# Gate and up of a hybrid block: stores issued from POOL's queue, raw weights asked for one projection ahead

## The chip, the core and the metric

The kernel runs on one core of a Trainium2 chip. Its time is device microseconds (us) of one execution. The engines are TensorE (PE, with its weight loads PEld), VectorE (DVE), ScalarE (ACT), GpSimd (POOL) and SyncE (SP). SP computes nothing here: it issues DMA transfers in the order of its program, and when an instruction waits on it, the ones behind wait too. POOL can issue transfers in the same way from a queue of its own.

## The reference

One layer of a trunk with two groups of heads, on 2048 tokens of width 1024. Here it is cut to the feed-forward part, in which the change lies; ahead of it a state-space layer and chunked attention share one input and one output projection.

```python
def rmsnorm(x, g):
    return x * lax.rsqrt(jnp.mean(x * x, axis=-1, keepdims=True) + EPS) * g

# D_MODEL = 1024, SEQ = 2048, D_FF = 2816
x = x + mixed @ w_out                       # x1 in the kernel
h = rmsnorm(x, norm_ffn_g)
x = x + (silu(h @ w_gate) * (h @ w_up)) @ w_down
out = rmsnorm(x, norm_final_g)
```

## The kernel before

Everything is float32. Each operand of a product is split into a high part (an ACT cast) and a low part (a DVE subtraction; `split`, L179), and three matmuls (high by high, low by high, high by low) make up one float32 product (`mm3`, L81 in the profile).

**Gate and up** (`gate_up_phase`) goes over two halves of 1024 tokens (`hf`), and in each over 11 pairs of 128-wide blocks of D_FF (`f`, with f + 11), for w_gate and then w_up: 44 *projections*. One projection is a 2 x 2 block product done with seven products instead of eight, called B11, T1, T2, B21, T3, B22 and T4. Their weight operands are made by DVE from two tiles of raw weights, r0 and r1 (512 KB each): sums in S tiles (five of them), split into c tiles (five). The token operands are hi0 to hi6 and lo0 to lo6, one pair for each product; for the second half they are loaded from a buffer in DRAM, `hc` (`build`, L1468), when the first half's last use of the tiles is over. Results gather in three kinds of PSUM banks, X, Y and W; ACT copies some to u tiles. A projection's work is in three parts, and the last part of one is done inside the next: `p.one()`, `before.three()`, `p.two()`.

The raw tiles come in turn from two pools, `k.gr` and `g2`: two pairs in all. Their loads are issued on SP when a `Proj` is made, and each waits for the last reader of the tile.

Beside the projections, a generator (`pre`) is moved on by one step a projection. It first makes the second half's token operands: `pre_steps` loads blocks of x into `px` tiles (four of them, L1428), scales and combines them on DVE, and stores the results to `hc` (L1421). Then `weight_steps` does the same with w_down: loads into px tiles (L1385), combines, and stores to `wc` (L1379). The gated product g (ten tiles) is combined and stored to `hq` (L1575), and the blocks listed in `TAILF` are stored to `hs` as they are (L1571). So hc, wc, hq and hs are buffers in DRAM that are written here and read later.

**Down** (`down_phase`) loads the `hq` and `wc` blocks as hd tiles (768 KB each, a pair for a product), splits them, multiplies into `ps` banks, and adds onto `acc`, tiles loaded from x. Of the first group of blocks, all 14 hd loads are issued from POOL (`aside`); later ones from SP. Their first loads and the acc loads begin while gate and up is ending.

The order on each engine is made by a scheduler from the order of the code; a tile's next user waits for its last reader.

Of the kernel before, what the change touches and what calls it, by code (L numbers as in the profile page):

```python
# [16 lines left out]
P = 128  # L17
# [44 lines left out]
F2 = NF // 2  # L62
# [8 lines left out]
TAILF = 9, 10, 20, 21  # L71
# [1289 lines left out]
def in_turn(n, load, first, second):  # L1361
    for q in range(n + 1):
        if q:
            second(q - 1)
        if q < n:
            load(q)
            yield
            first(q)
        yield


def weight_steps(k, S, tile, tile1):

    nc = k.nc
    V = nc.vector
    st = {}

    def put(f, n, a):
        nc.sync.dma_start(S["wc"][f, n], a[:])  # L1379

    def load(f):
        st[f] = []
        for r, c in ((0, 0), (0, 1), (F2, 0), (F2, 1)):
            a = tile()
            nc.sync.dma_start(a[:], k.io["w_down"][(f + r) * P : (f + r + 1) * P, c * 512 : (c + 1) * 512])  # L1385
            st[f].append(a)

    def first(f):
        a11, a21, a12, a22 = st[f]
        for n, a in ((B11, a11), (B21, a12), (T4, a22)):  # L1390
            put(f, n, a)
        s1 = tile1()
        V.tensor_tensor(s1[:], a21[:], a22[:], op=ALU.add)
        put(f, T1, s1)
        V.tensor_tensor(a21[:], a11[:], a21[:], op=ALU.subtract)
        put(f, T3, a21)
        st[f].append(s1)

    def second(f):
        a11, _, a12, _, s1 = st.pop(f)  # L1400
        V.tensor_tensor(a11[:], s1[:], a11[:], op=ALU.subtract)
        put(f, T2, a11)
        V.tensor_tensor(a12[:], a12[:], a11[:], op=ALU.subtract)
        put(f, B22, a12)

    for m, f in enumerate(TAILF):
        k.tc.keep_in_program_order(nc.sync.dma_start(S["wt"][m], k.io["w_down"][f * P : (f + 1) * P, :]))
    yield from in_turn(F2, load, first, second)


def pre_steps(k, S, hf, tile, deep, tile1=None):

    nc = k.nc
    V = nc.vector
    t0 = hf * HALF
    st = {}

    def put(q, n, b):  # L1420
        nc.sync.dma_start(S["hc"][hf, n, :, q], b)  # L1421

    def load(q):
        st[q] = []
        for r, c in ((0, 0), (0, 1), (4, 0), (4, 1)):
            b = tile()[:]
            ts = slice(t0 + c * 512, t0 + c * 512 + 512)
            nc.sync.dma_start(b, S["x1"][(q + r) * P : (q + r + 1) * P, ts])  # L1428
            st[q].append((b, q + r, ts))

    def first(q):
        for b, r, ts in st[q]:
            V.scalar_tensor_tensor(b, b, k.gf[:, r : r + 1], S["rsn"][:, ts], op0=ALU.mult, op1=ALU.mult)
        b11, b12, b21, b22 = st[q] = [b for b, _, _ in st[q]]
        for n, b in ((B11, b11), (B21, b21), (B22, b22)):
            put(q, n, b)
        t = (tile1 or tile)()[:]
        V.tensor_tensor(t, b12, b11, op=ALU.subtract)
        put(q, T1, t)
        V.tensor_tensor(b12, b22, b12, op=ALU.subtract)  # L1440
        put(q, T3, b12)
        st[q].append(t)

    def second(q):
        b11, b12, b21, b22, t = st.pop(q)
        V.tensor_tensor(b22, b22, t, op=ALU.subtract)
        put(q, T2, b22)
        V.tensor_tensor(b21, b21, b22, op=ALU.subtract)
        put(q, T4, b21)

    if deep:
        for q in range(6):
            for d, f in ((2, second), (1, first), (0, load)):
                if 0 <= q - d < 4:
                    f(q - d)
            yield
    else:
        yield from in_turn(4, load, first, second)


def build(k, S, hf, pool, ns):

    hT = {}
    for n in ns:
        hi, lo = hT[n] = tuple(k.t(pool, f"{m}{n}", [P, 4, 512], F32R) for m in ("hi", "lo"))
        with k.tc.high_priority():
            for q in range(4) if hf == 0 else (slice(0, 4),):
                k.nc.sync.dma_start(f32(lo[:, q]), S["hc"][hf, n, :, q])  # L1468
        for q in range(4):
            split(k, hi[:, q], lo[:, q], f32(lo[:, q]))  # L1470
    return hT


def gate_up_phase(k, S):

    tc, nc, io = k.tc, k.nc, k.io
    V, te = nc.vector, k.te
    with ExitStack() as cx:
# [9 lines left out]
        xr = rstd_steps(k, te, psum["X"], k.mf, ("X", [P, 512]), k.last, D, S["rsn"][:, (NSB - 1) * SB :])  # L1488

        raws = cycle((k.gr,) * 2 + (g2,) * 2)  # L1490

        class Proj:


            def __init__(self, hT, w, f, post):
                self.hT, self.post = hT, post
                r0, r1 = (k.t(next(raws), "raw", [P, 1024]) for _ in range(2))
                nc.sync.dma_start(r0[:], w[f])
                nc.sync.dma_start(r1[:], w[f + F2])
                self.a11, self.a12, a21, self.a22 = r0[:, :512], r0[:, 512:], r1[:, :512], r1[:, 512:]  # L1500

                def s(x, y, op):
                    o = k.t(gb, "S", [P, 512], bufs=SB_)
                    V.tensor_tensor(o[:], x, y, op=op)
                    return o[:]

                self.s1 = s(a21, self.a22, ALU.add)
                self.s2 = s(self.s1, self.a11, ALU.subtract)
                self.s3 = s(self.a11, a21, ALU.subtract)
                self.s4 = s(self.a12, self.s2, ALU.subtract)  # L1510
# [34 lines left out]
            def three(self):  # L1545
                self.product(B22, self.s4, self.y, False)
                self.add(self.u2, self.y, 0, 1)
                self.product(T4, self.a22, self.x, False)
                self.post(self.x, 1, 0)

        before = None
        tiles = (lambda: k.t(gp, "px", [P, 512])), (lambda: k.t(gb, "S", [P, 512], bufs=SB_))
        pre = chain(pre_steps(k, S, 1, tiles[0], False, tiles[1]), weight_steps(k, S, *tiles))
        for hf in range(2):
            hT = build(k, S, 1, k.ga1, EARLY) if hf else k.hT
            hT.update(build(k, S, hf, ga, LATE))
            for f in range(F2):
                gs = {}

                def gt():  # L1560
                    return k.t(gb, "g", [P, 512], bufs=GB_)

                def gate(u, r, c, gs=gs):
                    g = gs[r, c] = gt()
                    nc.scalar.activation(g[:], u[:], AF.Silu)

                def up(u, r, c, gs=gs, hf=hf, f=f):
                    g = gs[r, c]
                    V.tensor_tensor(g[:], g[:], u[:], op=ALU.mult)
                    if hf and f + r * F2 in TAILF:  # L1570
                        nc.sync.dma_start(S["h"][TAILF.index(f + r * F2), :, c * 512 : (c + 1) * 512], g[:])  # L1571
                        return

                    def put(n, b):
                        nc.sync.dma_start(S["hq"][hf, f, n], b[:])  # L1575

                    if (r, c) == (0, 0):
                        put(B11, g)
                    elif (r, c) == (1, 1):
                        put(B22, g)  # L1580
                    elif (r, c) == (0, 1):
                        t1, t2 = gt(), gt()
                        V.tensor_tensor(t1[:], g[:], gs[0, 0][:], op=ALU.subtract)
                        put(T1, t1)
                        V.tensor_tensor(t2[:], gs[1, 1][:], t1[:], op=ALU.subtract)
                        put(T2, t2)
                        V.tensor_tensor(g[:], gs[1, 1][:], g[:], op=ALU.subtract)
                        put(T3, g)
                        gs["t2"] = t2
                    else:  # L1590
                        put(B21, g)
                        t4 = gt()
                        V.tensor_tensor(t4[:], g[:], gs["t2"][:], op=ALU.subtract)
                        put(T4, t4)

                for w, post in (("w_gate", gate), ("w_up", up)):
                    p = Proj(hT, io[w], f, post)
                    p.one()
                    if before:
                        before.three()  # L1600
                    p.two()
                    before = p
                    if hf or f > 1:
                        next(pre, None)
                if hf == 0 and f < 2:
                    next(xr)
# [284 lines left out]
```

## Time and profile before

| | |
|---|---|
| median of 3 runs | 2211.99 us (2210.46 to 2216.73) |
| profiled execution, own time | 2214.67 us |
| its span | 2212.9 us |
| mean granted clock of PE | 0.992 |
| PE busy | 2155.7 us, 97% |
| DVE busy | 1534.3 us, 69% |
| ACT busy | 1008.1 us, 46% |
| POOL busy | 371.5 us, 17% |
| moved by the hardware queue (SP) | 404.05 MB |
| moved by the software queue (POOL) | 25.24 MB |

Times in the views are microseconds from the start of the span, which leaves some 1.8 us of the execution outside. In a timeline row stand start, length, engine, line, operation, output<-input and count, and in square brackets how long the engine was idle before and what it waited for. A merged row (x2 and more) runs to the end of its last instruction. In a row of stretches the granted clock (1.00 is full) stands behind the engines. SPq is SP's queue: the length of a row there is the issue, not the transfer.

### The profile page before, as it was taken

To read this page: it belongs to the slowest core of one execution; us is meant where nothing else is said; L and a number is where in the kernel's file an instruction comes from. 1 tells how busy PE (TensorE), PEld (TensorE's weight loads), DVE (VectorE), ACT (ScalarE), POOL (GpSimd) and SP (SyncE) were. 2 spreads that over 40 slices of the span, in tenths; PEclk is the share of its full clock that TensorE was granted. 3 is DMA by queue.
4 is the path that set the end of the run, shared out by engine and by line. 5 is a ranking of instruction groups with operands and counts; after the bars stand their busy time and mean duration, and the time that the engine had idled before them with its cause. 6 is when DMAs were issued, how large, how long until landed. Compare 5 with 4: busy or idle time off the path is not lost.

```text
span 2212.9 us, 30057 instructions
## 1 busy us (share of the span) xinstructions
PE 2155.7 (97%) x10606; PEld 1816.1 (82%) x10606; DVE 1534.3 (69%) x2667; ACT 1008.1 (46%) x1684; POOL 371.5 (17%) x839
## 2 busy tenths in 40 slices
PE   8999999999998999999999999999999999999998
PEld 6787898998977888788888887888888788888887
DVE  8767566565568657767776768767665477689785
ACT  6356566555677521533333345333333443354332
POOL 3367777676110000000000000000000100000000
PEclk9999999999999999999999999999999999999999
DMA  9788977665633346835555657545332395465552
GB/s 323 240 284 268 303 229 241 210 202 174 202 111 138 119 143 218 262 100 182 177 174 190 211 189 262 194 159 203 110 113 102 123 390 179 164 220 197 193 216 77
DMA packets 194423, 431.20 MB, mean 195 GB/s; under 512 B 19744, under 2 KB 37200, under 8 KB 187168
## 3 DMA queue, kind: packets, MB, share of 16 engines
q1 hardware_dynamic: 186448, 404.05, 54.7%
q0 software_dynamic: 7824, 25.24, 3.8%
q8 instruction: 83, 1.36, 0.3%
q14 instruction: 68, 0.56, 0.1%
HBM read 290.00 MB, written 131.10 MB: 190 GB/s over the span
## 4 chain that ended last, share of the span: by engine, by line
PE 61%; DMA 5%; DVE 2%; ACT 1%; issue 1%; SPq 0%; DVEq 0%; ACTq 0%
PE X L81 21%; PE ps L81 17%; PE Y L81 11%; PE big L81 6%; PE W L81 5%; DMA acc<-x 2%; DMA lo<-hc 1%; DMA x<-xt 1%; DVE xt L1239 0%; DMA hd<-wc 0%; DMA m<-in_w_out 0%; ACT hi L179 0%; DMA hc<-gh 0%; DVE acc L1664 0%; SPq L1134 0%
## 5 line engine op out<-in xcount | busy, mean ns | idle before, releaser
L81 PE MATMUL X<-hi,c 128*128 128x512 f32 x1408 | 451.7, 392 | 9.6 <-DVE c L179 5.0
L81 PE MATMUL ps<-hd,hd 128*128 128x512 f32 (+1 forms) x1920 | 428.8, 384 | 3.4 <-DVE hd L179 2.0
L81 PEld LDWEIGHTS ps<-hd,hd 128*128 128x128 f32 x1920 | 353.3, 188 | 75.1 <-DVE hd L179 2.7
L81 PEld LDWEIGHTS X<-hi,c 128*128 128x128 f32 x1408 | 265.8, 189 | 66.5 <-DVE c L179 5.9
L81 PE MATMUL X<-lo,c 128*128 128x512 f32 x704 | 275.3, 391 | 0.0
L179 ACT CAST hd<-hd 128x1536 fp32r<-128x1536 f32 (+1 forms) x106 | 147.5, 1394 | 230.7 <-DMA hd<-hq 164.9
L81 PE MATMUL Y<-hi,c 128*128 128x512 f32 x704 | 224.8, 390 | 1.5 <-DVE u L1526 1.5
L179 DVE TENSOR_TENSOR hd<-hd 128x1536 fp32r<-128x1536 f32 (+1 forms) x106 | 174.2, 1645 | 35.9 <-ACT hd L179 35.1
L179 DVE TENSOR_TENSOR c<-S,c 128x512 fp32r<-128x512 f32 x176 | 120.9, 688 | 101.0 <-ACT c L179 100.8
L1630 POOL DMA_DIRECT2D hd<-hq x7 | 5.2, 745 | 1072.0 <-PE X L81 1060.7
L1522 ACT COPY u<-X 128x512 f32<-128x512 f32 x132 | 77.4, 587 | 197.7 <-PE X L81 197.7
L179 ACT CAST c<-S 128x512 fp32r<-128x512 f32 x176 | 109.4, 622 | 121.7 <-PE Y L81 62.0
L81 PE MATMUL big<-m,woh 128*128 128x512 f32 x512 | 161.2, 396 | 0.0
L81 PEld LDWEIGHTS Y<-hi,c 128*128 128x128 f32 x704 | 132.7, 189 | 29.9 <-DVE u L1526 2.2
L1664 DVE TENSOR_TENSOR acc<-acc,ps 128x512 f32<-128x512 f32 x196 | 130.3, 683 | 38.5 <-PE ps L81 38.0
L81 PEld LDWEIGHTS X<-lo,c 128*128 128x128 f32 x704 | 132.9, 189 | 27.5
L179 ACT CAST c<-raw 128x512 fp32r<-128x512 f32 x132 | 82.2, 623 | 148.8 <-PE Y L81 73.0
L81 PE MATMUL pf<-hi,w 128*128 128x512 f32 x416 | 148.8, 410 | 0.0
L81 PE MATMUL Y<-lo,c 128*128 128x512 f32 x352 | 137.2, 390 | 0.0
L957 DVE TENSOR_TENSOR ptl<-pt,pth 128x640 fp32r<-128x640 f32 (+3 forms) x152 | 98.3, 646 | 46.1 <-ACT pth L956 42.1
L940 ACT ACTIVATE s<-s,mn 128x640 f32<-128x640 f32 (+4 forms) x128 | 97.9, 765 | 51.4 <-DVE mn L937 50.9
L956 ACT CAST pth<-pt 128x640 fp32r<-128x640 f32 (+3 forms) x152 | 83.8, 551 | 81.2 <-PE pt L84 75.7
(494 smaller groups left out, 4281.3 us busy)
## 6 DMA issues: line engine op xcount, KB each, us to landing
w<-wss SPq DMA_DIRECT2D x36, 1024.0 KB, 6.1
hq<-g SPq DMA_DIRECT2D x140, 256.0 KB, 2.1
hd<-hq SPq DMA_DIRECT2D x35, 768.0 KB, 4.4
hd<-wc SPq DMA_DIRECT2D x35, 768.0 KB, 5.9
raw<-in_w_gate SPq DMA_DIRECT2D x44, 512.0 KB, 3.6
raw<-in_w_up SPq DMA_DIRECT2D x44, 512.0 KB, 4.1
wc<-px SPq DMA_DIRECT2D x66, 256.0 KB, 3.1
wss<-w SPq DMA_DIRECT2D x12, 1024.0 KB, 6.3
```

Of the source, the lines that this page charges most:

```text
L81: return self.tc.keep_in_program_order(self.tc.nc.tensor.matmul(*a, **b))
L179: return nc.scalar.copy(hi, raw), nc.vector.tensor_tensor(lo, raw, f32(hi), op=ALU.subtract)
L940: nc.scalar.activation(s[:, :nk], s[:, :nk], AF.Exp, bias=mn[:], scale=-1.0, accum_out=sums[sb, pr][:, hh, qp : qp + 1])
L956: nc.scalar.copy(pth[:, a:b, qp, :], pt[:, a:b, :])
L957: k.low = nc.vector.tensor_tensor(ptl[:, a:b, qp, :], pt[:, a:b, :], f32(pth[:, a:b, qp, :]), op=ALU.subtract).ins
L1522: nc.scalar.copy(u[:], ps[:])
L1630: (nc.gpsimd if aside else nc.sync).dma_start(f32(lo), src.rearrange("g p c -> p g c"))
L1664: V.tensor_tensor(a, a, ps[:], op=ALU.add)
```

## The change

All stores in gate and up (wc, hc of the second half, hq, hs) are issued from POOL instead of SP. The raw weights of a projection are asked for by `load_next()`: once at the start, once behind the first `p.one()`, and from then on at the end of each `three()`; a `Proj` takes the pair that was loaded. The pools and the number of tiles are what they were.

```diff
 def weight_steps(...)
     def put(f, n, a):
-        nc.sync.dma_start(S["wc"][f, n], a[:])
+        nc.gpsimd.dma_start(S["wc"][f, n], a[:])
...
 def pre_steps(...)
     def put(q, n, b):
-        nc.sync.dma_start(S["hc"][hf, n, :, q], b)
+        (nc.gpsimd if hf else nc.sync).dma_start(S["hc"][hf, n, :, q], b)
...
 def gate_up_phase(k, S)
         raws = cycle((k.gr,) * 2 + (g2,) * 2)
+        wanted = iter([(io[n], f) for _ in range(2) for f in range(F2) for n in ("w_gate", "w_up")])
+        loaded = []
+
+        def load_next():
+            for w, f in islice(wanted, 1):
+                r0, r1 = (k.t(next(raws), "raw", [P, 1024]) for _ in range(2))
+                nc.sync.dma_start(r0[:], w[f])
+                nc.sync.dma_start(r1[:], w[f + F2])
+                loaded.append((r0, r1))
 
         class Proj:
-            def __init__(self, hT, w, f, post):
+            def __init__(self, hT, post):
                 self.hT, self.post = hT, post
-                r0, r1 = (k.t(next(raws), "raw", [P, 1024]) for _ in range(2))
-                nc.sync.dma_start(r0[:], w[f])
-                nc.sync.dma_start(r1[:], w[f + F2])
+                r0, r1 = loaded.pop()
...
             def three(self):
                 ...
                 self.product(T4, self.a22, self.x, False)
+                load_next()
                 self.post(self.x, 1, 0)
 
+        load_next()
         before = None
...
                     if hf and f + r * F2 in TAILF:
-                        nc.sync.dma_start(S["h"][...], g[:])
+                        nc.gpsimd.dma_start(S["h"][...], g[:])
                     ...
                     def put(n, b):
-                        nc.sync.dma_start(S["hq"][hf, f, n], b[:])
+                        nc.gpsimd.dma_start(S["hq"][hf, f, n], b[:])
...
-                for w, post in (("w_gate", gate), ("w_up", up)):
-                    p = Proj(hT, io[w], f, post)
+                for post in (gate, up):
+                    p = Proj(hT, post)
                     p.one()
                     if before:
                         before.three()
+                    else:
+                        load_next()
                     p.two()
```

The order of PE and of ACT is the same before and after. On DVE 28 instructions change places with a neighbour. SP's list goes from 1063 to 810 rows, POOL's from 815 to 1068: 253 stores. Lines move by up to 11 (hs L1580, hq L1584, raw L1497 and L1498, hd L1641, acc L1680 after).

On POOL, at the end of gate and up, stand first the loads of the down product's first group (hd, from hq and wc, in pairs). Before:

```order
L1630 DMA hd_16997<-hq_75 128x3x512
L1630 DMA hd_17001<-wc_76 128x3x512
L1630 DMA hd_17005<-hq_75 128x3x512
L1630 DMA hd_17009<-wc_76 128x3x512
L1630 DMA hd_17057<-hq_75 128x3x512
```

Now, with the numbers of the g tiles:

```order
L1580 DMA hs_73<-g_16511 128x512
L1580 DMA hs_73<-g_16571 128x512
L1580 DMA hs_73<-g_16592 128x512
L1580 DMA hs_73<-g_16765 128x512
L1641 DMA hd_16997<-hq_75 128x3x512
L1641 DMA hd_17001<-wc_76 128x3x512
L1641 DMA hd_17005<-hq_75 128x3x512
L1641 DMA hd_17009<-wc_76 128x3x512
L1580 DMA hs_73<-g_16785 128x512
L1580 DMA hs_73<-g_16845 128x512
L1580 DMA hs_73<-g_16862 128x512
L1641 DMA hd_17057<-hq_75 128x3x512
```

Five stores of hs (the first is left out) stand ahead of the first load, and three more between the fourth and the fifth.

On SP at the change of halves (lo: the second half's token operands, here lo4, lo5 and lo6). Before:

```order
L1468 DMA lo4_2617_13642<-hc_10_72 128x2048
L1575 DMA hq_13_75<-g_2578_13418 128x512
L1575 DMA hq_13_75<-g_2581_13438 128x512
L1379 DMA wc_14_76<-S_2646_13824 128x512
L1379 DMA wc_14_76<-px_2605_13591 128x512
L1499 DMA raw_2648_13830<-in_w_up 128x1024
L1468 DMA lo5_2619_13653<-hc_10_72 128x2048
L1468 DMA lo6_2621_13664<-hc_10_72 128x2048
```

Now:

```order
L1468 DMA lo_2619_13646<-hc_72 128x2048
L1498 DMA raw_13761<-in_w_up 128x1024
L1385 DMA px_13974<-in_w_down 128x512
L1385 DMA px_13976<-in_w_down 128x512
L1497 DMA raw_13908<-in_w_gate 128x1024
L1468 DMA lo_2621_13657<-hc_72 128x2048
L1468 DMA lo_2623_13668<-hc_72 128x2048
```

The four stores between lo4 and lo5 are gone, the load of w_up's r1 follows lo4, and two loads of px and the next projection's r0 have come ahead of lo5.

On SP in the first half, where x is loaded into px tiles while hc is stored. Before:

```order
L1421 DMA hc_72<-S_11460 128x512
L1421 DMA hc_72<-px_11310 128x512
L1428 DMA px_11616<-x_5_67 128x512
L1421 DMA hc_72<-px_11314 128x512
L1499 DMA raw_11466<-in_w_gate 128x1024
L1421 DMA hc_72<-px_11312 128x512
L1428 DMA px_11618<-x_5_67 128x512
L1428 DMA px_11620<-x_5_67 128x512
L1421 DMA hc_72<-px_11616 128x512
L1428 DMA px_11622<-x_5_67 128x512
```

Now:

```order
L1497 DMA raw_11395<-in_w_gate 128x1024
L1428 DMA px_11620<-x_5_67 128x512
L1498 DMA raw_11396<-in_w_gate 128x1024
L1428 DMA px_11622<-x_5_67 128x512
L1428 DMA px_11624<-x_5_67 128x512
L1428 DMA px_11626<-x_5_67 128x512
```

The loads stand in the order they had among themselves; the stores of hc that each waits for are on POOL.

More of the change, by code (lines that the diff above doesn't have):

```diff
@@ L1490, in gate_up_phase @@
         raws = cycle((k.gr,) * 2 + (g2,) * 2)
-        class Proj:
-            def __init__(self, hT, w, f, post):
-                self.hT, self.post = hT, post
+        wanted = iter([(io[n], f) for _ in range(2) for f in range(F2) for n in ("w_gate", "w_up")])
+        loaded = []
+        def load_next():
+            for w, f in islice(wanted, 1):
                 r0, r1 = (k.t(next(raws), "raw", [P, 1024]) for _ in range(2))
@@ L1499, in __init__ @@
                 nc.sync.dma_start(r1[:], w[f + F2])
+                loaded.append((r0, r1))
+        class Proj:
+            def __init__(self, hT, post):
+                self.hT, self.post = hT, post
+                r0, r1 = loaded.pop()
                 self.a11, self.a12, a21, self.a22 = r0[:, :512], r0[:, 512:], r1[:, :512], r1[:, 512:]
@@ L1570, in up @@
                     if hf and f + r * F2 in TAILF:
-                        nc.sync.dma_start(S["h"][TAILF.index(f + r * F2), :, c * 512 : (c + 1) * 512], g[:])
+                        nc.gpsimd.dma_start(S["h"][TAILF.index(f + r * F2), :, c * 512 : (c + 1) * 512], g[:])
                         return
                     def put(n, b):
-                        nc.sync.dma_start(S["hq"][hf, f, n], b[:])
+                        nc.gpsimd.dma_start(S["hq"][hf, f, n], b[:])
                     if (r, c) == (0, 0):
```

## The prediction

> **What bounds the kernel now.** I read the stretches of the part that the change touches first, then who TensorE (PE) waits for in it, and last the timeline at the few places where it waits.
>
> Three stretches of gate and up, which runs from about 915 to 1768 us, with the down product behind it; the columns are start and end, length, the busy time and the count of PE, PE's weight loads, DVE, ACT and POOL, then granted clock, DMA share, GB/s:
>
> ```profile
> 990.00:1080.00 90.00, 90.00 (x401) 74.55 (x400) 67.86 (x107) 32.04 (x56) 0.00 (x0) 1.00 0.55 174
> 1320.00:1360.00 40.00, 35.27 (x154) 28.61 (x153) 37.52 (x62) 27.01 (x50) 0.00 (x0) 1.00 0.84 306
> 1360.00:1500.00 140.00, 140.00 (x612) 115.72 (x612) 95.87 (x148) 50.69 (x87) 0.00 (x0) 0.99 0.56 188
> ```
>
> In the first and the last, which are steady, PE is busy for their whole length at the full clock, with DMA about half used; the middle one is the change from the first half of the tokens to the second. What PE waits for between 880 and 1775 us (total, times, longest):
>
> ```profile
> PE X L81 <- DVE c L179: 5.0, 2, 3.4
> PE X L81 <- DVE xt L1239: 3.3, 1, 3.3
> PE ps L81 <- DVE hd L179: 2.0, 2, 1.8
> PE Y L81 <- DVE u L1526: 1.5, 1, 1.5
> PE X L81 <- ACT u L1522: 1.4, 1, 1.4
> ```
>
> These are 13.2 us, all at the start of gate and up, at the change of halves (1318 to 1363) and at the start of the down product. No wait ends with raw weights or a store. So 0.3%, 6.6 us here and about what a measurement of this kernel can tell from no change, can only be won if half of these waits go; there is more room to lose.
>
> **The change, part by part.** *The stores.* 253 stores of 256 KB move: 140 hq, 77 wc, 28 hc, 8 hs. On SP each takes about 0.32 us, on POOL, by the row of its loads below, 0.75. SP loses 253 x 0.32 = 81 us of issue and POOL gets 253 x 0.75 = 190 us, over some 850 us. POOL did nothing there (its 0.00 in the stretches), and PE's instructions keep their order, so neither is on the path. What can matter is when a store lands, since its tile is then free. Times from issue to landing (count, KB, median us):
>
> ```profile
> hq<-g SPq DMA_DIRECT2D x140, 256.0 KB, 2.1
> ...
> hc<-px SPq DMA_DIRECT2D x24, 256.0 KB, 4.3
> ...
> u<-us POOLq DMA_DIRECT2D x16, 256.0 KB, 4.9
> ```
>
> No store from POOL's queue is in this part of the trace. The nearest row is a load of the same size from that queue, 4.9; the stores on SP give 2.1 to 4.3. I take a store 1 to 3 us later for POOL, and cover below. The g tiles (ten) and S tiles (five) have room for that; the four px tiles have not: x is loaded into one as soon as the store of its last content has landed. The second of three such places in the first half, on SP:
>
> ```profile
> 1045.67 0.45 SPq L1428 DMA_DIRECT2D px<-x  x1
> ...
> 1049.08 3.15 SPq L1428 DMA_DIRECT2D px<-x  x2
> ```
>
> on DVE and on PE:
>
> ```profile
> 1051.28 0.75 DVE L1433 SCALAR_TENSOR_TENSOR px<-px,g_ffn,rsn 128x512 f32<-128x512 f32 x1 [3.00 <-DMA px<-x]
> ...
> 1052.55 0.69 DVE L179 TENSOR_TENSOR c<-S,c 128x512 fp32r<-128x512 f32 x1
> ```
>
> ```profile
> 1054.71 0.61 PE L81 MATMUL Y<-hi,c 128*128 128x512 f32 x2
> ```
>
> DVE waits 3.00 us for the load issued at 1045.67; behind it stands the low part c of a product's operand, ready at 1053.24, read by PE in the row at 1054.71. The cover is 1.5 us. The load at 1045.67 stood on SP behind stores of hc, which are gone: it can go about 1 us sooner. The next loads need the stores at POOL, at 0.75 each and a later landing: 1 to 2 us later than at 1049.08, but they are used behind the c. So 0, with bounds of -0 (PE isn't waiting) and, if the landing is worse, rival 1.
>
> *The raw weights.* They have two pairs of tiles before and after, so a load still waits for the DVE instruction that last reads the tile; asking one projection ahead doesn't give a third pair. SP's order shows them in nearly the old places among the loads. PE never waits for them: 0.
>
> *The change of halves.* SP there, then ACT, then PE with the stretch behind its second gap:
>
> ```profile
> 1339.64 0.40 SPq L1499 DMA_DIRECT2D raw<-in_w_up  x1
> 1342.54 3.04 SPq L1468 DMA_DIRECT2D lo<-hc  x2
> ```
>
> ```profile
> 1349.56 2.18 ACT L179 CAST hi<-lo 128x512 fp32r<-128x512 f32 x4 [0.37 <-DMA lo<-hc]
> ```
>
> ```profile
> 1352.27 0.50 PE L81 MATMUL X<-hi,c 128*128 128x512 f32 x1 [1.38 <-ACT u L1522]
> ...
> 1359.09 0.78 PE L81 MATMUL X<-hi,c 128*128 128x512 f32 x2 [3.35 <-DVE c L179]
> ```
>
> ```profile
> 1359.09:1363.08 3.99, 3.99 (x11) 3.13 (x12) 2.96 (x5) 0.00 (x0) 0.00 (x0) 0.57 0.28 79
> ```
>
> The load of lo5 at 1342.54 waits for the old half's last product, not for SP: ACT gets to casting it 0.37 us after it could, and PE's gaps of 1.38 and 3.35 follow from there, the second through a run of DVE work without a pause. After the change two loads of px and a raw load of 0.5 MB stand right ahead of lo5 on SP, and the raw load waits for a DVE split of c. That split stands on DVE for the same last product, so I reckon that it is done at about 1342.5 and that lo5, with the raw load's 0.32 to 0.4 us of issue ahead of it, goes some 0.4 us later. In the old order another 0.5 MB was in flight there (1339.64). Bounds: -0.5, if that makes lo5's 7 us shorter, to +2. I take **+0.4**.
>
> *The start of the down product.* This is where the order changes most. In this order: POOL's loads of hd; a store of hs and the loads of acc on SP; ACT; DVE; PE; and the stretch in which the first loads would now land.
>
> ```profile
> 1744.38 0.76 POOL L1630 DMA_DIRECT2D hd<-hq  x1 [1060.75 <-PE X L81]
> 1755.50 0.75 POOL L1630 DMA_DIRECT2D hd<-wc  x1 [10.35 <-PE X L81]
> ...
> 1766.93 0.74 POOL L1630 DMA_DIRECT2D hd<-hq  x1 [8.21 <-issue]
> ```
>
> ```profile
> 1759.16 0.32 SPq L1571 DMA_DIRECT2D hs<-g  x1
> 1759.57 1.91 SPq L1669 DMA_DIRECT2D acc<-x  x3
> ```
>
> ```profile
> 1760.97 4.22 ACT L179 CAST hd<-hd 128x1536 fp32r<-128x1536 f32 x3
> ```
>
> ```profile
> 1766.24 1.75 DVE L179 TENSOR_TENSOR hd<-hd 128x1536 fp32r<-128x1536 f32 x1
> ...
> 1768.50 3.42 DVE L179 TENSOR_TENSOR hd<-hd 128x1536 fp32r<-128x1536 f32 x2
> ```
>
> ```profile
> 1768.04 0.50 PE L81 MATMUL ps<-hd,hd 128*128 128x512 f32 x1 [0.23 <-DVE hd L179]
> 1770.31 57.00 PE L81 MATMUL ps<-hd,hd 128*128 128x512 f32 x250 [1.76 <-DVE hd L179]
> ```
>
> ```profile
> 1770.00:1780.00 10.00, 9.69 (x42) 7.99 (x43) 8.06 (x9) 2.96 (x2) 0.67 (x1) 1.00 1.04 412
> ```
>
> Now five hs stores stand on POOL ahead of the first hd load. The fifth waits for the DVE multiply whose store SP issued at 1759.16. With 0.75 a piece the four first hd loads go at 1759.9, 1760.65, 1761.4 and 1762.15, where the first two went at 1744.38 and 1755.50. These two (1.5 MB) land in a stretch in which DMA already moves 412 GB/s: 1.5/0.41 = 3.7 us. The acc loads, no longer behind stores, start some 2 us sooner and take part of that. For the first pair I reckon half of the rate for POOL's queue at worst and all of it at best: 0.75 MB at 412 GB/s is 1.8 us, at half 3.7, and some 2 us of latency. The first lands at 1763.7 to 1765.7, the second at 1765.5 to 1769.3. Take 1765 and 1767.9. The cast takes 4.22/3 = 1.4 us, the split 1.75 (3.42/2 = 1.7): the second operand's cast ends at 1769.3 and its low part at 1771.1 to 1771.6, by the order on DVE, where a multiply stands between. PE went on at 1770.31. That is **+1.2**, from -0.5 to +2.5.
>
> PE then has a gap of nearly 4 us in one or two pieces instead of 0.23 and 1.76. After 1.38 and 3.35 the granted clock was 0.57: ten matmuls from 1359.09 to the next at 1363.08 took 3.99 us, where 401 take 90 in the first stretch above, so 3.99 - 2.24 = 1.75, say 1.8, were lost. After 0.23 and 1.76 nothing is lost. I take half, **+0.9**. The Trainium skill ("TensorE: Matmul & The Clock Gate", "What's actually happening") has the clock halved only after an idle window of about 3.4 us; with two shorter gaps it would be 0 here and the sum 1.6. The 3.35 after 1.38 speaks for counting them together.
>
> The sum: 0.4 + 1.2 + 0.9 = +2.5 us on the profiled execution's 2214.67, so 2217.2. That execution is 2.7 over the median of 2211.99; against the median it is **2214.5**.
>
> **The rivals.** *1. POOL's stores land late (slower).* If the DVE work beside it (68 of 90 us in the first stretch) holds up POOL's transfers, each px load comes later by what its store takes longer, at three places for x (w_down goes through the same tiles, and DVE doesn't wait for it now). The point from which it decides is the cover of 1.5 us. With 4 us more, PE stands still 2.5 x 3 = 7.5 us, and with the +2.5 the kernel takes 2222; past 1.5 + 4.1/3 = 2.9 us it is out of the 0.3%, and with a clock lost each time it would be 2227. For it: the medians 2.1 and 4.9 differ by 2.8. Against it: in the trace POOL issues hd loads in 0.74 to 0.76 whether DVE is idle (1744.38) or in its splits (1766.93). Chance 0.2. The Trainium skill ("SBUF — State Buffer", "SBUF: two separate sides") speaks for this rival: a transfer from POOL has its descriptors written by POOL's cores, which DVE locks out of their shared port while it runs certain fast copies. This case's rows show no longer issue beside DVE, but no store.
>
> *2. DMA paces the start of the down product (slower).* The 3.7 us of moved bytes also delay the later pairs, and the loads behind the eighth hs store (1766.93 before) go at about 1770.4. If POOL's queue only gets half of 412 GB/s while acc loads, a pair of 1.5 MB takes 7.5 us, about what PE takes for a product (250 matmuls in 57 us, 36 a product: 8.2). Then the first gap is +2.5, one or two later ones +1.5 each, and the clock is lost once or twice at 1.8: 0.4 + 2.5 + 2.3 + 2.7 = about +8, 2220. For it: DMA share 1.04. Against it: the pairs behind have several us in hand before. Chance 0.18.
>
> *3. The change of halves gets better (faster).* If SP, free of stores, has the raw weights in earlier and the pause of 1.38 and the one of 3.35 with its slow clock of 1.8 go, that is -6.5, 2205.5. For it: the raw load at 1339.64 would go at about 1335. Against it: the chain there starts from lo5 and a busy DVE. Chance 0.12, with whatever else makes it faster.
>
> *4. It does nothing.* All is hidden, the start of the down product too: 2212. It lies within 0.3%, chance 0.15.
>
> **How the numbers follow.** My forecast has 0.35; with rival 4, same is 0.5. Slower is 1 and 2: 0.38; faster 0.12. The time is 2214.5. For 8 in 10 I leave out the better part of rival 3 and the upper half of rival 1: 2207 to 2225. The forecast alone, with its bounds of -1 (-0.5 - 0.5) and +6.3 (2 + 2.5 + 1.8), is 2211 to 2218.3.
>
> **What would show it.** Right: PE at 90.00 of 90.00 in the steady stretches; the first hd load at 1760 on POOL (same clock of the span) and PE's wait for DVE hd risen from 2.0 to 3 or 4 us; the stores on POOL landing in 3 to 5 us; lo5 issued just after the last old product. Wrong: PE waits for c once a projection pair in the first half (rival 1), waits for hd in several places up to 1810 (rival 2), or the gap of 3.35 gone (rival 3). A steady stretch under 99% busy would mean that I have missed a tile whose store is needed sooner than I saw.

## The result and the profile after

The changed kernel takes 2223.27 us (median of 7 runs, 2222.13 to 2228.66) where the kernel before takes 2216.73 in its runs beside it (7 runs, 2210.46 to 2219.57): a ratio of 1.0037, 95% interval 1.0027 to 1.0048. That is some 8 us slower by the ratio; the two medians are 6.5 us apart. The profiled execution takes 2224.77 us, its span is 2223.0; against the profiled execution of before that is +10.1.

Stretches of the changed kernel, columns as in those of before:

```profile
990.00:1080.00 90.00, 90.00 (x401) 74.55 (x400) 67.97 (x107) 32.38 (x56) 17.36 (x32) 1.00 0.50 173
...
1320.00:1360.00 40.00, 36.80 (x151) 29.80 (x149) 33.84 (x55) 25.07 (x47) 5.96 (x11) 0.92 0.81 305
1360.00:1500.00 140.00, 136.88 (x597) 113.00 (x596) 95.89 (x149) 51.03 (x88) 27.61 (x51) 0.99 0.51 177
1500.00:1680.00 180.00, 180.00 (x795) 149.07 (x795) 117.60 (x182) 66.17 (x113) 25.45 (x47) 1.00 0.39 137
```

POOL now has work in every stretch, and PE is as full as before in the steady ones. Only the change of halves has less in it: fewer matmuls up to 1360 (151 instead of 154), and the second gap now falls behind 1360 (136.88 of 140.00). At that place and at the start of the down product PE's rows are now:

```profile
1354.18 0.79 PE L81 MATMUL X<-hi,c 128*128 128x512 f32 x1 [3.20 <-ACT u L1529]
...
1363.47 1.22 PE L81 MATMUL X<-hi,c 128*128 128x512 f32 x2 [3.12 <-DVE c L179]
...
1776.97 1.22 PE L81 MATMUL ps<-hd,hd 128*128 128x512 f32 x2 [5.07 <-ACT hd L179]
1778.77 59.09 PE L81 MATMUL ps<-hd,hd 128*128 128x512 f32 x250 [0.57 <-DVE hd L179]
1839.47 20.91 PE L81 MATMUL ps<-hd,hd 128*128 128x512 f32 x91 [1.61 <-DVE acc L1675]
```

Up to the first gap the two executions run within 0.2 us of one another. There the gap is 3.20 instead of 1.38 (+1.8). The matmuls from its end to the second gap take 1360.35 - 1354.18 = 6.17 us, where they took 1355.74 - 1352.27 = 3.47: the clock is lost a first time (+2.7). The second gap is 0.2 shorter. That makes +4.3. At the down product the matmul at 1778.77 stood at 1770.31: +8.5, so some +4.1 beyond the 4.3; and the 250 matmuls behind it take 59.09 instead of 57.00, +2.1. Together 10.5, and 0.4 comes back later.

The stores of the changed kernel in gate and up (count, KB, median us from issue to landing):

```profile
hq<-g POOLq DMA_DIRECT2D x140, 256.0 KB, 2.7
...
wc<-px POOLq DMA_DIRECT2D x66, 256.0 KB, 3.3
...
hc<-px POOLq DMA_DIRECT2D x24, 256.0 KB, 4.7
```

and who DVE waits for there (total, times, longest):

```profile
DVE px L1433 <- DMA px<-x: 2.3, 3, 1.6
```

A store from POOL lands 0.2 to 0.6 us later than the same one did from SP in the views of before (2.1, 3.1 and 4.3). The px loads, which had stood behind stores on SP, now let DVE wait 2.3 us in all, where it had waited 12.3.

### The profile page after: what moved, and what is told of

It reads as the page before. It is cut to its first block, busy times and chain, and to the rows that moved or that the text cites. A ratio compares the mean times of both kernels' runs of the same rounds, so it can differ in the third digit from the quotient of the medians.

```text
span 2223.0 us, 30233 instructions
## 1 busy us (share of the span) xinstructions
PE 2161.8 (97%) x10606; PEld 1820.9 (82%) x10606; DVE 1530.4 (69%) x2667; ACT 1008.9 (45%) x1684; POOL 509.3 (23%) x1092
## 4 chain that ended last, share of the span: by engine, by line
PE 61%; DMA 4%; DVE 3%; ACT 1%; issue 1%; SPq 0%; DVEq 0%; ACTq 0%
PE X L81 21%; PE ps L81 18%; PE Y L81 10%; PE big L81 6%; PE W L81 5%; DMA lo<-hc 1%; DMA x<-xt 1%; DMA hd<-wc 0%; DVE hd L179 0%; DMA hd<-hq 0%; DVE xt L1239 0%; DMA m<-in_w_out 0%; DMA gl<-x 0%; DMA hc<-gh 0%; DVE acc L1675 0%
## 5 line engine op out<-in xcount | busy, mean ns | idle before, releaser
L81 PE MATMUL X<-hi,c 128*128 128x512 f32 x1408 | 453.8, 393 | 10.5 <-DVE c L179 4.8
L1584 POOL DMA_DIRECT2D hq<-g x140 | 75.9, 542 | 325.9 <-DVE g L1578 175.8
```

Source lines behind the costliest of these rows:

```text
L81: return self.tc.keep_in_program_order(self.tc.nc.tensor.matmul(*a, **b))
L1584: nc.gpsimd.dma_start(S["hq"][hf, f, n], b[:])
```

## The experiments

The theory: the change costs time through the places of a few transfers in two queues. On POOL the first hd loads stand behind the fifth hs store; on SP, with the stores gone, a raw load stands right ahead of lo5. The rivals: stores on POOL's queue cost something as such, or asking for raw weights ahead does.

**1. Only asking ahead, all stores back on SP.**

```diff
-        nc.gpsimd.dma_start(S["wc"][f, n], a[:])        # and hc, hq, hs alike
+        nc.sync.dma_start(S["wc"][f, n], a[:])
```

> The changed kernel with all stores back on SP; only the raw weights are still asked for one projection ahead. My theory is that both losses come from places in the queues: on SP a raw load stands ahead of lo5 because the stores are gone, on POOL the hd loads stand behind hs stores. Here SP has its stores again and the raw load stands behind lo6, so the time is that of before within 2 us, PE's gaps at the change of halves are 1.4 and 3.4, at the down product 0.2 and 1.8. A rival, that asking ahead itself disturbs the change of halves, gives +4 us over before, with a first gap of about 3.2 there.

Measured: 1.0001 (0.9992 to 1.0011); gaps of 0.89 and 3.47 at the change of halves, 0.23 and 1.77 at the down product. Asking ahead does nothing that the comparison shows; there are two pairs of tiles either way.

**2. Only the stores on POOL**, the raw loads as before (the same four lines of stores changed in the kernel before).

> The kernel before with all stores on POOL; the raw weights are asked for as before. My theory (places in the queues) gives all of the loss: +8 to +10 us over before, gaps of about 3.2 and 3.1 at the change of halves and of 5 at the down product, the same as the changed kernel within 2 us. The rival that asking ahead makes the loss at the change of halves gives only +6.

Measured: 1.0035 (1.0021 to 1.0048), gaps of 3.52 and 3.34, then 5.65. All of the loss comes with the stores. The raw load stands right ahead of lo5 here too (1341.55 and 1341.97 on SP): what brings it there is that the stores are gone from SP.

**3. and 4. hs back on SP in the changed kernel; only hs on POOL in the kernel before.**

```diff
-                        nc.gpsimd.dma_start(S["h"][...], g[:])      # 3, in the changed kernel
+                        nc.sync.dma_start(S["h"][...], g[:])
```

> The changed kernel with the eight hs stores back on SP; all other stores stay on POOL. My theory: nothing stands ahead of the hd loads on POOL now, they go at their old times (some 16 and 5 us sooner than in the changed kernel), the 5 us gap goes back to under 2.5 and the clock isn't lost there: 6 us less than the changed kernel, some +4 over before, all of it at the change of halves. The rival, that the loss at the down product comes from the many transfers of POOL's queue as such, leaves at least 4 of the 6 us.

> The kernel before with only the eight hs stores on POOL. My theory: the hd loads wait behind the fifth of them, PE has a gap of about 5 us at the start of the down product and loses the clock there: +6 over before; the change of halves is as before (1.4 and 3.4). The rival gives at most +2, since POOL's queue carries only eight stores.

Measured: with hs on SP 0.9994 (0.9984 to 1.0004), with hs alone on POOL 1.0022 (1.0012 to 1.0032). So eight stores of 253 make most of the loss, and without them 245 stores on POOL cost nothing that this comparison shows (experiments 6 and 9 come back to that). PE with hs on SP, then with hs alone on POOL:

```profile
1771.57 0.51 PE L81 MATMUL ps<-hd,hd 128*128 128x512 f32 x1 [0.23 <-DVE hd L179]
1773.84 56.97 PE L81 MATMUL ps<-hd,hd 128*128 128x512 f32 x250 [1.76 <-DVE hd L179]
```

```profile
1775.03 1.22 PE L81 MATMUL ps<-hd,hd 128*128 128x512 f32 x2 [7.75 <-ACT hd L179]
1776.82 58.49 PE L81 MATMUL ps<-hd,hd 128*128 128x512 f32 x250 [0.57 <-DVE hd L179]
```

The first has the gaps of before, 0.23 and 1.76, and 250 matmuls at full clock; the second has the long gap and the lost clock, with one kind of store moved.

**5. Why the first hd load takes 8.3 us.** POOL and ACT in the changed kernel:

```profile
1763.74 0.54 POOL L1580 DMA_DIRECT2D hs<-g  x1 [24.66 <-DVE g L1578]
1764.29 0.77 POOL L1641 DMA_DIRECT2D hd<-hq  x1
1765.04 0.77 POOL L1641 DMA_DIRECT2D hd<-wc  x1
...
1772.57 1.47 ACT L179 CAST hd<-hd 128x1536 fp32r<-128x1536 f32 x1 [7.17 <-DMA hd<-hq]
1775.45 1.47 ACT L179 CAST hd<-hd 128x1536 fp32r<-128x1536 f32 x1 [1.41 <-DMA hd<-wc]
```

POOL waits 24.66 us for the g of the fifth hs store, and the first hd load goes behind it, 4.4 us later than the 1759.9 that I had reckoned, which is about what was lost at the change of halves. What was reckoned too short is its landing: 1764.29 to 1772.57. In two runs I tried to take the acc loads from beside it. The first issues those of the first half from POOL:

```diff
-                nc.sync.dma_start(acc[i][...], S["x1"][...])
+                (nc.sync if hf else nc.gpsimd).dma_start(acc[i][...], S["x1"][...])
```

> The changed kernel with the first half's 16 acc loads issued from POOL too, behind the hd loads and hs stores there, instead of from SP where they start before the hd loads. In the changed kernel the first hd load takes 8.2 us to land, where I had reckoned 5.1. If the acc loads beside it are the cause, it lands in 5 to 6 us now, the gap of 5.1 at the start of the down product becomes 2 to 3, and the time is 2 to 3 us less than the changed kernel's (2221). The rival is that the hd loads themselves, four at once behind one store, share what there is: then the gap stays above 4.5 and the time at 2223 to 2225.

Measured: 1.0056 (1.0038 to 1.0074). On SP the second half's acc loads moved up, 13 from 1758.53 on. The first hd load took 6.1 us (1764.36 to the cast at 1770.51) and the gap fell from 5.07 to 3.65; the time rose nevertheless, since acc and hd loads then waited for one another on POOL, and PE waited for hd at three later places, 1796, 1823 and 1825. The second run holds the first acc load back, behind which the others were meant to stand:

```diff
+            if not hf and (r, c) == (0, 0):
+                nc.scalar.copy(acc[0][:, 0:1], f32(ops[B11][1][0][:, 0, 0:1]))
```

> The changed kernel with the acc loads held on SP until the second hd operand (the first wc block) has been cast: ACT copies one column of it into the first acc tile, which the load then overwrites. In the run with the first half's acc loads on POOL, those of the second half moved up on SP and stood beside the hd loads again, so that run left the question open. Here no acc load is beside the first hd loads. If acc is what makes the first hd load take 8.2 us in the changed kernel, it lands in 5 to 6 now, the second in about 7, and the gap of 5.1 becomes 2 to 3; the time falls by at most 2 us, since the acc loads come later. The rival, that four hd loads behind one another need that long alone, keeps 8 us and a gap of 4.5 or more.

Measured: 1.0035 (1.0022 to 1.0048), first landing 8.3 us, gap 5.02. The scheduler put the other acc loads ahead of the held one, from 1764.29 on, so they stood beside the hd loads again; this run decides nothing. What can be read is what each queue moves (q0 is POOL's, q1 SP's; packets, MB, share of the DMA engines' time) while the first hd load is under way. Before, its third hd load, 1757.24 to 1763.2, 5.9 us:

```profile
q0 software_dynamic: 498, 1.91, 95.2%
q1 hardware_dynamic: 1, 0.00, 0.1%
```

with the acc loads partly elsewhere (acc on POOL), 6.1 us; in the changed kernel, 8.3; with the first acc load held back, 8.3; with hs alone on POOL, 9.5:

```profile
q0 software_dynamic: 295, 1.08, 57.8%
q1 hardware_dynamic: 220, 0.42, 22.5%
```

```profile
q0 software_dynamic: 358, 1.34, 48.2%
q1 hardware_dynamic: 658, 1.20, 46.7%
```

```profile
q0 software_dynamic: 394, 1.48, 56.4%
q1 hardware_dynamic: 582, 1.06, 40.2%
```

```profile
q1 hardware_dynamic: 966, 1.76, 58.9%
q0 software_dynamic: 395, 1.49, 38.5%
```

Where SP's queue moves 0.42 MB or less meanwhile, the load lands in about 6 us; where it moves 1.06 to 1.76 MB, in 8.3 to 9.5. POOL's share of the engines' time doesn't order them: 57.8% goes with 6.1 us, 56.4% with 8.3. A longer landing leaves more time for SP's queue to move bytes, so this doesn't prove that the acc loads delay it; a kernel without acc loads there was not run. Nor has the first hd load POOL's queue to itself. Of the 1.34 MB in the changed kernel it is 0.79 (768 KB); the rest are hs stores and the hd loads behind it. Both queues together moved 309 GB/s there.

**6. All hd loads on SP, hs on POOL.**

```diff
-                (nc.gpsimd if aside else nc.sync).dma_start(f32(lo), ...)
+                nc.sync.dma_start(f32(lo), ...)
```

> The changed kernel with all hd loads on SP, the hs stores staying on POOL. If only the place behind the hs stores costs the 6 us, the hd loads go at their old times (1744 and 1756 of before), the gaps at the down product are below 2.5 and the time is that with hs on SP, 2216. The rival, that hs on POOL and the acc loads that start sooner cost something by themselves, leaves 2 us or more of the loss.

Measured: 1.0016 (1.0004 to 1.0027). The gaps at the down product are 0.23 and 1.76, and PE has no pause behind them up to 1900 us, where this view ends:

```profile
1771.36 0.51 PE L81 MATMUL ps<-hd,hd 128*128 128x512 f32 x1 [0.23 <-DVE hd L179]
1773.62 126.55 PE L81 MATMUL ps<-hd,hd 128*128 128x512 f32 x557 [1.76 <-DVE hd L179]
```

So hs on POOL is harmless there when no hd load stands behind it. On SP the hd loads stand ahead of the acc loads too, so this run doesn't tell the two apart. The remaining 0.16% is not at that place in its profile. The matmul at 1773.62 is 3.3 us later than before, but 2.8 of them were lost before the first moved store (PE's first wait of gate and up ends at 917.41 instead of 914.64). Its change of halves has a first gap of 2.21.

**7. The raw load ahead of lo5** (with hs on SP).

```diff
+                if k.nload == 2 * F2 + 2:
+                    nc.gpsimd.tensor_copy(r0[:, 0:1], f32(hT[T4][0][:, 3, 0:1]))
                 nc.sync.dma_start(r0[:], w[f])
```

> The kernel with hs on SP, and the raw weights of the third projection of the second half (w_gate, r0 and r1) held back until lo6 has landed and been cast, by a one-column copy on POOL from hi6 into r0; nothing else reads that column. If the raw load of 0.5 MB right ahead of lo5 delays it, lo5 lands in 5.5 to 6.5 us instead of 8, the first gap at the change of halves goes from 3.2 to 1.4 or less, and the time is 2 to 4 us below the kernel with hs on SP (2212 to 2214). The rival, that lo5 is held by lo6 and the stores beside it, leaves the gap above 2.5 and the time at 2216.

Measured: 1.0004 (0.9993 to 1.0014). On SP in the changed kernel the raw load goes right ahead of lo5 and lo6:

```profile
1342.59 0.33 SPq L1497 DMA_DIRECT2D raw<-in_w_gate  x1
1343.01 2.67 SPq L1468 DMA_DIRECT2D lo<-hc  x2
```

The loads of lo5 and lo6 between 1335 and 1352 (before, changed, this run):

```profile
lo<-hc SPq DMA_DIRECT2D x2, 1024.0 KB, 6.9
```

```profile
lo<-hc SPq DMA_DIRECT2D x2, 1024.0 KB, 9.0
```

```profile
lo<-hc SPq DMA_DIRECT2D x2, 1024.0 KB, 7.9
```

Without the raw load beside them they land about 1 us sooner than in the changed kernel, and the first gap goes to 1.77. That is about half of the 2.1 us by which they are later than before; the rest stays with what else is in flight there (two px loads, the stores on POOL), which no run took apart. But the second gap goes to 4.38: DVE now has lo6's four splits ahead of both u, and behind those stand the sums and the c for which PE waits. So the two gaps sum to 6.15 (6.32 in the changed kernel). The load was a cause of the first gap; the time didn't follow.

**8. Three sums ahead of the splits** (the kernel of 7, with `tc.high_priority()` around that projection's four S sums).

> As the one before, and the four S sums of the second projection of the second half are given priority on DVE, so that three of them stand ahead of the splits of lo5 and lo6 instead of behind (they wait for raw weights that are there by then). If the run of DVE work behind lo6 makes the second gap of 3.3, it shrinks by three sums, 1.8 us, to about 1.5, and the clock isn't lost there (another 1.8): 2 to 3.5 us less than the one before, 2210 to 2212, which would beat the kernel before. The rival: the sums only push lo5's splits and the u behind them later; the two gaps together stay the same, and so does the time.

Measured: 1.0007 (0.9996 to 1.0017), gaps 1.50 and 5.20. A miss: DVE waits 2.17 us for the raw weights at the first sum and the rest moves behind, lo5's and lo6's splits included.

**9. The changed kernel, and the one with hs on SP, once more.**

> The changed kernel once more, on the chip of the next run. 1.0037 of the kernel before, within 0.0015; the gaps at the two places as before (3.2 and 3.1; 5.1 and 0.6), the clock lost in some of them only.

> The changed kernel with hs on SP once more. Its profile showed 4 us lost at the change of halves, its first comparison no loss against the kernel before (0.9994). If the loss at the change of halves is in most executions, the ratio is 1.0010 to 1.0020 now and the gaps are 3.2 and 3.2 again; if it was the luck of one execution, the ratio is 1.000 or below, and the gaps differ from the first profile's.

Measured: 1.0035 (1.0020 to 1.0050) and 1.0005 (0.9996 to 1.0015). The changed kernel shows the same gaps (3.41 and 3.15; 5.00 and 0.57), and the clock lost again at both places. With hs on SP the second profile has these gaps:

```profile
1351.89 0.50 PE L81 MATMUL X<-hi,c 128*128 128x512 f32 x1 [2.71 <-ACT u L1529]
1360.25 1.22 PE L81 MATMUL X<-hi,c 128*128 128x512 f32 x2 [3.29 <-DVE c L179]
```

The first matmul runs at full speed (0.50), but the clock is lost about 1 us later: the 14 matmuls between the gaps take 1360.25 - 3.29 - 1351.89 = 5.07 us, where they take 3.47 before and 6.11 in the first profile of this kernel. So the longer first gap is there in every profile with wc, hc and hq on POOL (2.2 to 3.5 us) unless the raw load is held back, and what it costs varies. From the start of the first gap to the end of PE's next wait behind both, for a u (1761.85 before, 1766.17 in the changed kernel), the changed kernel's two profiles take 4.2 and 4.4 us more than before, those with hs on SP 4.2 and 2.7, the one with the hd loads on SP 0.7. In time, 0.9994 and 1.0005 leave 0 to 2 us for the change of halves with hs on SP, and 1.0016 with the hd loads on SP leaves some 3.5; why these don't agree with the profiles, or with one another, stays open.

**10. lo5 and lo6 in quarters, in the kernel before.**

```diff
-            for q in range(4) if hf == 0 else (slice(0, 4),):
+            for q in range(4) if hf == 0 or n in LATE else (slice(0, 4),):
```

> The kernel before, all stores on SP, with lo5 and lo6 loaded in four quarters each instead of whole at the change of halves. If PE's first gap there comes from waiting for the whole 1 MB of lo5 (7 us), the first quarter lands in 3 to 5 us, casts and splits start sooner and both gaps shrink: 2 to 4 us less than before (0.998 to 0.999). The rival: ACT and DVE need what comes last anyway, and SP holds lo5's last quarter behind lo6's first ones: no difference, or up to 2 us more.

Measured: 0.9989 (0.9980 to 0.9998), 2212.99 us: some 2 us faster than the kernel before, though the interval only just ends below 1, and clearly faster than the changed one. Its loads, in the same stretch, and ACT and PE at the change of halves:

```profile
lo<-hc SPq DMA_DIRECT2D x8, 256.0 KB, 4.2
```

```profile
1347.00 1.34 ACT L179 CAST hi<-lo 128x512 fp32r<-128x512 f32 x2 [2.48 <-DMA lo<-hc]
```

```profile
1358.20 0.73 PE L81 MATMUL X<-hi,c 128*128 128x512 f32 x2 [3.01 <-DVE c L179]
1358.77 0.40 PE L81 MATMUL X<-lo,c 128*128 128x512 f32 x1
1359.00 0.62 PE L81 MATMUL X<-hi,c 128*128 128x512 f32 x2
```

A quarter lands in 4.2 us, the casts begin at 1347.00 instead of 1349.56, and the first gap is gone. The second alone, 3.01, didn't cost the clock: matmuls follow every 0.23 us. From PE's first wait of gate and up (914.64 before, 916.08 here) to the down product (1770.31, 1767.83) this profile takes 3.9 us less.

## Why the prediction was right, and where its terms were off

The time is in the range, 2207 to 2225, but the forecast itself missed. With its own bounds it ended at +6.3, 2218.3; measured are +6.5 by the medians and +8 by the ratio. The kernel before itself stood at 2216.73 in the runs beside it, 4.7 us over the median from which I had reckoned. So 2223.27 is inside only because the range had room for the slower rivals. It came out slower by over 0.3%, by the ratio (its interval begins at 0.27%); I gave that side 0.38 and held no measurable change the likeliest (0.5). That rival 2 had the same +8 is luck in part: it put 0.4 us at the change of halves, where the profile shows 4.3, and its later waits at the down product did not come.

- *Steady stretches, stores, raw weights:* as forecast. PE at 90.00 of 90.00; asking ahead 1.0001; the stores 0.2 to 0.6 us later, less than the 1 to 3 that I had taken. Rival 1 fell with that: DVE's wait for px went from 12.3 to 2.3 us, not up. The Trainium skill's rule about DVE locking out POOL's transfers ("SBUF — State Buffer", "SBUF: two separate sides") shows no trace here: POOL issued stores in 0.54 to 0.56 us, and DVE was as busy as before, 67.97 of 90.
- *The change of halves, +0.4:* lo5 went late as reckoned (0.4 to 0.5 us), but the step "another 0.5 MB was in flight there" failed. The old one had been issued 2.9 us ahead of lo5, the new one right ahead of it. lo5 and lo6 took 9.0 us instead of 6.9, about half of it by the raw load (experiment 7): a gap of +1.8, at the edge of my bound of +2, and with it the clock, +2.7, which I had not priced at this place at all.
- *The down product, +1.2:* the issue of the first hd load was right to 0.1 us once 4.3 is added. The landing was not: at most 5.8 us by my bounds, it took 8.3. POOL's queue got 48% of the engines' time, near my worst case of half. But the engines moved 309 GB/s, not 412, and of the 2.54 MB only 0.79 were the first load's, for which I had reckoned the whole of POOL's part. That put the term at +4.1, over its end of +2.5.
- *The clock, +0.9:* 2.1 measured. A gap's length doesn't settle it. In two runs PE went on like this, with the acc loads on POOL and with the hd loads on SP:

```profile
1356.26 0.50 PE L81 MATMUL X<-hi,c 128*128 128x512 f32 x1 [3.30 <-ACT u L1529]
...
1363.47 0.73 PE L81 MATMUL X<-hi,c 128*128 128x512 f32 x2 [3.75 <-DVE c L179]
```

```profile
1355.67 0.80 PE L81 MATMUL X<-hi,c 128*128 128x512 f32 x1 [2.21 <-ACT u L1529]
...
1364.01 0.73 PE L81 MATMUL X<-hi,c 128*128 128x512 f32 x2 [3.35 <-DVE c L179]
```

After 3.30 us the 14 matmuls up to the next gap took 3.46, full speed; after 2.21 they took 4.99. The speed of the first matmul alone doesn't tell: with only the stores moved it was full (0.50) behind a gap of 3.52, and the clock was lost 1.1 us later. The Trainium skill ("TensorE: Matmul & The Clock Gate", "What's actually happening") has the window of about 3.4 us run free, so that a gap's place in it counts; a 2.21 us gap that loses the clock is shorter than its rule of one idle window gives.

- *What I had called wrong signs:* further waits for hd up to 1810 did not come, so rival 2 held in its first gap and its lost clock, not in its later ones. PE's wait for hd rose to 5.6 us (5.07 and 0.57), not to 3 or 4.

## What to carry to other kernels

Before moving a store to an idle queue, look at what is already issued there and waits at its end: here a load that had gone 16 us ahead of need was put behind a store that waits for the last results. Where a queue is relieved, ask also what moves up into the place and shares the engines with the transfer that the next stage waits for. And a transfer that ends a stage's wait may be worth cutting into the pieces in which it is used, as in experiment 10.

## What the runs showed that I had not expected

The same kernel's executions spread over some 12 us (the kernel before: 2208.95 to 2221.34), and within its runs the time goes with the granted clock: in one set, 2218.4 on average at 0.989, 2214.6 at 0.992. A few gaps of 2 to 4 us that lose the clock or don't would be enough for that, each worth 1.6 to 2.7 us here; that they are the cause was not tested. In the profiles, PE's first wait of gate and up, ahead of any moved store, ends anywhere from 913.16 to 917.72. So a comparison of two single profiles across the whole kernel can be off by more than what one place loses, and each place is better measured from a row just ahead of it.
